# Splitting k and v at position 256, moving normalised x by 36 floats, and reordering work around it, in a stick-breaking decoder layer

## The chip, the cores and the metric

The kernel runs on one core of one Trainium2 chip. The metric is the device time of one execution in microseconds; the median of several runs counts.

## The reference

One decoder layer on 512 positions of 2048 channels, with 16 learned meta positions ahead of them, all in float32. `L` is 528.

```python
n = rmsnorm(h, g_mix)                       # (528, 2048)
q, k, v, gb, gc, u = split(n @ w_in)        # 1024 columns each
q, k = rmsnorm(q per head), rmsnorm(k per head)      # 8 heads x 128
z = q @ k.T / sqrt(128)                     # per head, strictly causal
log_pass = reverse_cumsum(log_sigmoid(-z)) - log_sigmoid(-z)
o_attn = exp(log_sigmoid(z) + log_pass) @ v
o_conv = gb * causal_dwconv(gc * u, 3 taps)
h = h + concat(rmsnorm(o_attn), rmsnorm(o_conv)) @ w_out
n2 = rmsnorm(h, g_ffn)
h = h + (silu(n2 @ w_gate) * (n2 @ w_up)) @ w_down   # 5632 wide
return h[16:]
```

## The kernel before

**Arithmetic.** Channels lie on the 128 partitions, positions on the free axis. Each float32 operand of a large product is split into a high part (`fp32r`, by ScalarE: a copy or `L201`, `L314`, `L372`) and the rest (by VectorE: `L202`, `L315`, `L373`). Each 128 x 128 block of a product takes three matmuls: high by high, high by rest, rest by high (`L301` to `L303`, `L778` to `L780`). The conv, gate/up and down products also save one multiplication in eight by a block scheme (seven block products in place of eight), which needs sums and differences of activations and of weights (`add_quads`, `L208`).

**Stages.** First q of head 0 and k of head 0 run side by side while x arrives and is split (`steps`), then v of head 0, then for heads 1 to 7: k, q, v. Attention of head h (`attend`) is spread between the k tiles of the next head's products by `after(n, work)`: work is called after n ticks, and a product gives a tick per k tile. Then channel group products of the conv stage, the output projection, the FFN's gate and up products, and the down products in four chunks.

**Weights.** `next_w` gives a product its next split weight piece and prepares pieces ahead (`prepare`: cast on ScalarE, subtract on VectorE, then the DMA issue on SyncE for the piece that will use the freed place). The first ten pieces are small ("first"), the following ones hold 8 k tiles ("wide"). `n_first` is 10; `S_AHEAD` is 2.

**Normalised x.** `n_parts` holds 32 tiles (high and rest of 16 k tiles), each of 576 floats; the position axis starts 4 floats into the tile. q reads positions 16 to 528, k and v read 0 to 264 and 264 to 528, each into a half of a two-bank PSUM tile. `halves` and `two` give the reads of both halves as one instruction. The PSUM pool `pp` has two such tiles, taken in turn.

**Mix steps.** The conv stage needs mixed blocks of x: `load_mix(k)` loads four blocks of 258 positions of the k tiles k and k + 8 into the tile `x_mix` (one buffer) by four DMAs on GpSimd's queue; `mix_x` scales them on ScalarE (`L460`), forms four differences on VectorE (`L462` to `L465`), splits them into two staging tiles and stores these to `mix_dram` by GpSimd's queue (`L470`). Staging tiles have two buffers, shared with the attention output of the heads (`st_o`). Before the conv stage `mix_dram` is loaded back (`L717`, `L750`).

**Order.** A planner takes the program with its own costs of each instruction and fills each engine's queue, by program order as priority; it can put an instruction far ahead of its place. `tc.high_priority()` raises a block; `tc.keep_in_program_order(i)` pins an instruction behind everything written before it for the same engine; `tc.issue_after(i)` puts what the block writes for i's engine behind i. Engines run their queues in order.

**End of the output projection.** For each output tile `residual`, `mixed_blocks` and `split_f` make the FFN's operands `acts`; the last tile (`i == KT - 1`) is on the way to the first FFN product. `h_scale` computes the FFN's norm within the first pair, its sum over channels on TensorE at `L661`.

## Time and profile before

| | |
|---|---|
| median of 3 runs | 2051.3 us (2051.23 to 2053.13) |
| profiled execution | 2049.99 us, its span 2048.3 us |
| granted TensorE clock over the span | 0.998 |
| busy: TensorE, VectorE, ScalarE, GpSimd | 99%, 85%, 52%, 19% |
| DMA traffic | 356.29 MB, mean 174 GB/s |

Rows of the timeline are: start in us from the span's start, duration, engine, line, operation, tile written and tiles read, shapes, count, and in brackets the idle time of the engine before it with what ended it. The views by line give busy us, mean ns of one, and idle time before. Stretches give, after the bounds, the length and then busy us and instruction count of PE, PEld, DVE, ACT and POOL, the granted clock, the DMA share and GB/s. PE is TensorE's matmul, PEld its weight load, DVE VectorE, ACT ScalarE, POOL GpSimd, SP SyncE.

### The profile page before, as it was taken

The page shows a single profiled execution, that of the slowest core. Times are in us where ns is not written, and L with a number is a line of the kernel's source. Part 1 is how long each engine was busy: PE and PEld are TensorE (multiplying, and loading weights), DVE is VectorE, ACT ScalarE, POOL GpSimd, SP SyncE. Part 2 cuts the span into 40 slices and gives each one's busy share as a digit, 9 for nine tenths or more (in the row PEclk, how much of TensorE's full clock was granted, in tenths as well). Part 3 has the DMA queues.
Part 4 walks back from the last instruction along what each step waited for, and adds up shares of the span by engine and source line. Part 5 has one row for each costly group of instructions (what it writes and reads, how often), then busy time and mean ns, then how long its engine had stood idle before and what let it go on. Part 6 is the DMA issues. An engine that isn't in the chain of part 4 may idle for free.

```text
span 2048.3 us, 39668 instructions
## 1 busy us (share of the span) xinstructions
PE 2031.4 (99%) x16134; PEld 1966.7 (96%) x16134; DVE 1743.4 (85%) x2227; ACT 1066.5 (52%) x1535; POOL 382.8 (19%) x571
## 2 busy tenths in 40 slices
PE   9999999999999999999999999999999999999999
PEld 8989999999998888999999999999999999999999
DVE  8878887688887778999888888988988978888888
ACT  7666666444454435555555555555555544444443
POOL 1122222200004441111011011111111242131211
PEclk9999999999999999999999999999999999999999
DMA  7243343643355555556465465465455899798864
GB/s 261 83 134 120 118 134 125 222 139 103 114 187 171 168 167 181 156 174 176 149 175 159 141 176 163 136 176 170 135 173 167 264 343 347 177 305 206 215 149 93
DMA packets 153287, 356.29 MB, mean 174 GB/s; under 512 B 13888, under 2 KB 63808, under 8 KB 152336
## 3 DMA queue, kind: packets, MB, share of 16 engines
q1 hardware_dynamic: 67456, 212.50, 32.1%
q0 software_dynamic: 85648, 141.26, 25.7%
q8 instruction: 126, 2.06, 0.4%
q14 instruction: 57, 0.47, 0.1%
HBM read 275.78 MB, written 77.92 MB: 173 GB/s over the span
## 4 chain that ended last, share of the span: by engine, by line
PE 89%; DMA 4%; DVE 3%; issue 1%; ACT 1%; POOL 1%; SPq 0%; DVEq 0%; ACTq 0%; POOLq 0%
PE x L778 13%; PE x L779 13%; PE x L780 13%; PE z L778 6%; PE z L779 6%; PE z L780 6%; PE y L778 3%; PE y L780 3%; PE y L779 3%; PE pv L301 1%; PE pv L302 1%; PE pv L303 1%; DMA sw_in<-w_down 1%; PE pq L303 1%; PE pq L301 1%
## 5 line engine op out<-in xcount | busy, mean ns | idle before, releaser
L201 ACT CAST sw_split<-sw_in 128x1024 fp32r<-128x1024 f32 (+2 forms) x668 | 662.1, 992 | 715.9 <-PE z L779 188.6
L202 DVE TENSOR_TENSOR sw_split<-sw_in,sw_split 128x1024 fp32r<-128x1024 f32 (+2 forms) x668 | 770.0, 1153 | 153.1 <-ACT sw_split L201 145.7
L778 PE MATMUL x<-f,sw_split 128*128 128x256 f32 x1408 | 388.3, 276 | 0.2 <-ACT sides L802 0.2
L780 PE MATMUL x<-f,sw_split 128*128 128x256 f32 x1408 | 387.9, 276 | 0.1
L779 PE MATMUL x<-f,sw_split 128*128 128x256 f32 x1408 | 387.9, 275 | 0.0
L778 PEld LDWEIGHTS x<-f,sw_split 128*128 128x128 f32 x1408 | 265.0, 188 | 0.6 <-ACT sides L802 0.4
L780 PEld LDWEIGHTS x<-f,sw_split 128*128 128x128 f32 x1408 | 264.9, 188 | 0.4 <-DVE sw_split L202 0.4
L779 PEld LDWEIGHTS x<-f,sw_split 128*128 128x128 f32 x1408 | 265.0, 188 | 0.1
L1032 POOL DMA_DIRECT2D fd<-s x147 | 103.7, 918 | 713.6 <-DVE s L315 691.6
L208 DVE TENSOR_TENSOR sw_in<-sw_in 128x1024 f32<-128x1024 f32 (+1 forms) x164 | 187.9, 1146 | 12.0 <-DMA sw_in<-w_gu 3.2
L779 PE MATMUL z<-f,sw_split 128*128 128x256 f32 x704 | 193.7, 275 | 1.9 <-DVE f L315 1.9
L778 PE MATMUL z<-f,sw_split 128*128 128x256 f32 x704 | 193.7, 275 | 1.0 <-ACT sides L800 1.0
L780 PE MATMUL z<-f,sw_split 128*128 128x256 f32 x704 | 193.6, 275 | 0.0
L780 PE MATMUL x<-ring,sw_split 128*128 128x256 f32 x608 | 167.3, 275 | 0.5 <-DVE sw_split L202 0.5
L778 PE MATMUL x<-ring,sw_split 128*128 128x256 f32 x608 | 167.2, 275 | 0.0
L779 PE MATMUL x<-ring,sw_split 128*128 128x256 f32 x608 | 167.2, 275 | 0.0
L779 PEld LDWEIGHTS z<-f,sw_split 128*128 128x128 f32 x704 | 132.2, 188 | 2.0 <-DVE f L315 2.0
L778 PEld LDWEIGHTS z<-f,sw_split 128*128 128x128 f32 x704 | 132.1, 188 | 1.2 <-ACT sides L800 1.2
L780 PEld LDWEIGHTS z<-f,sw_split 128*128 128x128 f32 x704 | 132.2, 188 | 0.0
L780 PEld LDWEIGHTS x<-ring,sw_split 128*128 128x128 f32 x608 | 114.1, 188 | 0.7 <-DVE sw_split L202 0.7
L778 PEld LDWEIGHTS x<-ring,sw_split 128*128 128x128 f32 x608 | 114.1, 188 | 0.0
L779 PEld LDWEIGHTS x<-ring,sw_split 128*128 128x128 f32 x608 | 114.1, 188 | 0.0
(611 smaller groups left out, 5511.9 us busy)
## 6 DMA issues: line engine op xcount, KB each, us to landing
sw_in<-w_gu SPq DMA_DIRECT2D x176, 512.0 KB, 3.9
sw_in<-w_in SPq DMA_DIRECT2D x92, 512.0 KB, 3.3
fd<-s POOLq DMA_DIRECT2D x147, 256.0 KB, 5.2
sw_in<-w_down SPq DMA_DIRECT2D x96, 384.0 KB, 4.4
ring<-fd POOLq DMA_DIRECT2D x42, 768.0 KB, 16.6
sw_in<-w_out SPq DMA_DIRECT2D x32, 512.0 KB, 3.5
out_T<-d POOLq DMA_DIRECT2D x54, 256.0 KB, 5.6
mix_dram<-st_x POOLq DMA_DIRECT2D x32, 258.0 KB, 2.9
```

The costliest lines, as they stand in the source:

```text
L201: sc.copy(hi, src)
L202: ve.tensor_tensor(lo, src, hi.bitcast(F32), ALU.subtract)
L208: return ve.tensor_tensor(sums[name], a, b, ALU.add)
L301: pe.matmul(ps, wh, ah[:, a:b], start=k + i == 0, stop=False)
L302: pe.matmul(ps, wh, al[:, a:b], start=False, stop=False)
L303: pe.matmul(ps, wl, ah[:, a:b], start=False, stop=k + i == last)
L778: pe.matmul(p, hi[:, kk], ah, start=start and j == k == 0, stop=False, skip_group_check=skip)
L779: pe.matmul(p, hi[:, kk], al, start=False, stop=False, skip_group_check=skip)
L780: pe.matmul(p, lo[:, kk], ah, start=False, stop=k == n - 1, skip_group_check=skip)
L1032: gp.dma_start(fd[c][s][:, :, k], t[:, :, i])
```

## The change

Normalised x starts 40 floats into its tiles in place of 4. k and v (and k's sum of squares) are cut into positions 0 to 256 and 256 to 528; the first part goes to the second half of the first PSUM bank, the second part to the start of the next bank, so that both lie side by side and are read as one run of 528. Weight pieces 11 and 12 (from 0) are prepared after the reads of q of head 0 have been put into ScalarE's queue. The load of the first mix step is written after head 1's product and pinned there, each following load at the end of the mix step before it; mix step k is written in head k + 2 in place of k + 1, and steps 6 and 7 in the first two conv products. The last two splits of the last output tile are raised like the rest of that tile's work.

```diff
@@ -269,9 +269,15 @@
                     load_quad(SIX + 1, QUADS[1])
 
     def next_w():
-        ahead = max(min(n_first, used[0] + 6), used[0] + 1 + S_AHEAD - (used[0] == n_first))
+        ahead = max(min(n_first, used[0] + 6), used[0] + 1 + S_AHEAD)
+        if used[0] < n_first:
+            ahead = min(ahead, n_first + 1)
         while len(split_w) < min(len(pieces), ahead):
-            prepare()
+            if n_first < len(split_w) <= n_first + S_AHEAD:
+                with tc.issue_after(read_q0[3].ins):
+                    prepare()
+            else:
+                prepare()
         used[0] += 1
         return split_w[used[0] - 1]
 
@@ -340,7 +346,7 @@
 
 
     H = L // 2
-    n_parts = [[npool.tile([P, L + 48], F32R, name=f"{t}{k}")[:, 4:] for t in ("nh", "nl")] for k in range(KT)]
+    n_parts = [[npool.tile([P, L + 48], F32R, name=f"{t}{k}")[:, 40:] for t in ("nh", "nl")] for k in range(KT)]
     npool.tile([P, 52], F32, name="pad_n")
     n_hl = []
     accs = [rpool.tile([P, L], F32, name=f"acc_x{i}") for i in range(2)]
@@ -381,8 +387,11 @@
             sc.activation(s, xts[k], AF.Square)
             ve.tensor_tensor(accs[k % 2], accs[k % 2], s, ALU.add)
 
-    def halves(ps, n):
-        return ps[:, :, :n]
+    def flat(ps):
+        return ps.rearrange("p a b -> p (a b)")[:, T2 : T2 + L]
+
+    def parts_of_all(ps):
+        return [(ps[:, 0, T2:], 0, T2), (ps[:, 1, : L - T2], T2, L)]
 
     def two(t):
         return t.rearrange("p (a b) -> p a b", a=2)
@@ -391,15 +400,14 @@
 
         raw = t512(L, "e", 2)[:, :cols]
         s = t512(L, "e2", 2)[:, :cols]
-        raw_v, s_v = (raw, s) if cols == SEQ else (two(raw), two(s))
-        sc.activation(s_v, ps, AF.Square)
-        last = sc.activation(raw_v, ps, AF.Copy, scale=g)
+        sc.activation(s, ps, AF.Square)
+        last = sc.activation(raw, ps, AF.Copy, scale=g)
         return raw, s, cols, last
 
     pk0 = pp.tile([P, 2, 512], F32, tag="pp", name="pk0")
     pq0 = pp.tile([P, 2, 512], F32, tag="pp", name="pq0")
     steps = [
-        product_steps([(pk0[:, 0, :H], 0, H), (pk0[:, 1, :H], H, L)], n_hl, KT),
+        product_steps(parts_of_all(pk0), n_hl, KT),
         product_steps([(pq0[:, 0, :], META, L)], n_hl, KT),
     ]
 
@@ -417,7 +425,7 @@
             split_x(k)
         for step in steps:
             next(step)
-    read_k0, read_q0 = read_qk(halves(pk0, H), g_k, L), read_qk(pq0[:, 0, :], gq_s, SEQ)
+    read_k0, read_q0 = read_qk(flat(pk0), g_k, L), read_qk(pq0[:, 0, :], gq_s, SEQ)
     for k in range(6):
         square_x(k)
     with tc.issue_after(read_k0[3].ins):
@@ -447,15 +455,19 @@
     def stage(name):
         return stpool.tile([P, 4 * N], F32R, tag="st_o", bufs=2, name=name)
 
+    xs = {}
+
     def load_mix(k):
-        x = xpool2.tile([P, 4, N], F32, tag="x", name=f"x_mix{k}")
+        xs[k] = xpool2.tile([P, 4, N], F32, tag="x", name=f"x_mix{k}")
         for m in range(4):
             at = C0 + m % 2 * T2
-            gp.dma_start(x[:, m], xT[k + m // 2 * 8][:, at : at + N])
-        return x
-
-    def mix_x(k, x):
-
+            load = gp.dma_start(xs[k][:, m], xT[k + m // 2 * 8][:, at : at + N])
+            if not k:
+                tc.keep_in_program_order(load)
+
+    def mix_x(k):
+
+        x = xs[k]
         for i in range(2):
             sc.activation(x[:, 2 * i : 2 * i + 2], x[:, 2 * i : 2 * i + 2], AF.Copy, scale=g_mix[:, k + 8 * i : k + 8 * i + 1])
         a0, a1, b0, b1 = (x[:, m] for m in range(4))
@@ -468,13 +480,15 @@
             split(st[:, :, 0], st[:, :, 1], x[:, m : m + 2])
             for i, block in enumerate(blocks):
                 gp.dma_start(mix_dram[block][:, k], st[:, i])
+        if k < 7:
+            load_mix(k + 1)
 
     def qk_norm(read, dst, parts_of, name):
 
         raw, s, cols = read[:3]
         sh = apool.tile([P, L], F32R, tag="sh", name=f"sh_{name}")[:, :cols]
         sl = apool.tile([P, L], F32R, tag="sl", name=f"sl_{name}")[:, :cols]
-        cuts = [(0, cols)] if cols == SEQ else [(0, H), (H, L)]
+        cuts = [(0, cols)] if cols == SEQ else [(0, T2), (T2, L)]
         split(sh, sl, s)
 
         def finish():
@@ -500,30 +514,31 @@
 
         if h:
             pk = pp.tile([P, 2, 512], F32, tag="pp", name=f"pk{h}")
-            product([(pk[:, 0, :H], 0, H), (pk[:, 1, :H], H, L)], n_hl)
-        read = read_qk(halves(pk, H), g_k, L) if h else read_k0
+            product(parts_of_all(pk), n_hl)
+        read = read_qk(flat(pk), g_k, L) if h else read_k0
         kn = kns[0]
         kh = apool.tile([P, 384], F32R, tag="kh", name=f"kh{h}")
         kl = apool.tile([P, 384], F32R, tag="kl", name=f"kl{h}")
         after(8 if h else 19, qk_norm(read, kn[:, :L], (kh, kl, 384), f"k{h}"))
 
         if h:
-            x = load_mix(h - 1)
             pq = pp.tile([P, 2, 512], F32, tag="pp", name=f"pq{h}")
             product([(pq[:, 0, :], META, L)], n_hl)
         read = read_qk(pq[:, 0, :], gq_s, SEQ) if h else read_q0
         qn = apool.tile([P, SEQ], F32, tag="qn", name=f"qn{h}")
         qh = apool.tile([P, SEQ], F32R, tag="qh", name=f"qh{h}")
         ql = apool.tile([P, SEQ], F32R, tag="ql", name=f"ql{h}")
-        if h:
-            after(5, lambda: mix_x(h - 1, x))
+        if h > 1:
+            after(5, lambda: mix_x(h - 2))
         after(9 if h else 22, qk_norm(read, qn, (qh, ql, SEQ), f"q{h}"))
 
         pv = pp.tile([P, 2, 512], F32, tag="pp", name=f"pv{h}")
-        product([(pv[:, 0, :H], 0, H), (pv[:, 1, :H], H, L)], n_hl)
+        product(parts_of_all(pv), n_hl)
         vt = t512(L, "e", 2)
         with tc.high_priority(0 if h else 1 << 20):
-            ve.tensor_tensor(two(vt[:, :L]), halves(pv, H), two(r), ALU.mult)
+            ve.tensor_tensor(vt[:, :L], flat(pv), r, ALU.mult)
+        if h == 1:
+            load_mix(0)
         after(6 if h else 15, lambda: attend(h, kn, kh, kl, qn, qh, ql, vt))
 
     def attend(h, kn, kh, kl, qn, qh, ql, vt):
@@ -680,8 +695,8 @@
         square_sum(acc_c, p, j == 0, s, ve)
         sc.activation(p, p, AF.Copy, scale=g_cnv[:, j : j + 1])
 
-    x = load_mix(7)
-    after(3, lambda: mix_x(7, x))
+    after(3, lambda: mix_x(6))
+    after(19, lambda: mix_x(7))
     pc = cu_product("pc0")
     cu0 = t512(L, "e", 2)[:, : SEQ + 2]
     ve.tensor_tensor(cu0[:, :T2], pc[:, 0, :T2], r2[:, C0 : C0 + T2], ALU.mult)
@@ -976,8 +991,8 @@
                 residual(ve)
                 mixed_blocks()
                 square_sum(acc_h, hj, False, wide_tmp("h", bufs=2), ve)
-            split_f(3, 5)
-            split_f(4, 6)
+                split_f(3, 5)
+                split_f(4, 6)
         else:
             residual(gp if half else ve)
             if half:
```

## The prediction

> **What bounds the kernel now.** First the page: the span, the busy shares, the chain that ended last.
>
> ```profile
> span 2048.3 us, 39668 instructions
> PE 2031.4 (99%) x16134; PEld 1966.7 (96%) x16134; DVE 1743.4 (85%) x2227; ACT 1066.5 (52%) x1535; POOL 382.8 (19%) x571
> PE 89%; DMA 4%; DVE 3%; issue 1%; ACT 1%; POOL 1%; SPq 0%; DVEq 0%; ACTq 0%; POOLq 0%
> ```
>
> TensorE sets the time: 99% busy and 89% of the chain. So an edit pays in two ways only: matmuls follow each other more closely, or a gap of TensorE (and the slow clock behind it) goes. Matmul ends are modelled, so I read pace from start to start in the timeline of PE, between two rows of a stretch without gaps.
>
> ```profile
> 35.07 0.28 PE L301 MATMUL pv<-nh,sw_split 128*128 128x264 f32 x1
> ...
> 43.81 0.28 PE L301 MATMUL pv<-nh,sw_split 128*128 128x264 f32 x1
> ...
> 387.18 0.39 PE L301 MATMUL pb<-nh,sw_split 128*128 128x512 f32 x1
> ...
> 397.58 0.39 PE L301 MATMUL pb<-nh,sw_split 128*128 128x512 f32 x1
> ...
> 614.54 0.39 PE L757 MATMUL po0z<-oc_hi,sw_split 128*128 128x512 f32 x1
> ...
> 617.26 0.39 PE L757 MATMUL po0z<-oc_hi,sw_split 128*128 128x512 f32 x1
> ...
> 902.78 0.28 PE L778 MATMUL z<-f,sw_split 128*128 128x256 f32 x1
> ...
> 905.50 0.28 PE L778 MATMUL x<-f,sw_split 128*128 128x256 f32 x1
> ```
>
> Steps between them: 72, 45, 12 and 24. So k and v's 264 columns take 8.74/72 = 121.4 ns, normalised x's 512 columns 10.40/45 = 231.1 ns, the output projection's 512 columns 2.72/12 = 226.7 ns, the FFN's 256 columns 2.72/24 = 113.3 ns. Per column: 0.460, 0.451, 0.443, 0.443. The first two read normalised x; the others do not. In the program of before, weights start at byte 128 modulo 256, the output projection's operands at 128, the FFN's at 240; k and v's two parts start at 176 and 208, q at 240. The change adds 36 floats: q comes to 128, equal to its weights, and both new parts of k and v to 64.
>
> **The change part by part.** Counts first, from the groups by line and the rows of the tile pb; then one row of the conv stage.
>
> ```profile
> L301 PE MATMUL pk<-nh,sw_split 128*128 128x264 f32 x256 | 73.9, 289 | 0.2 <-ACT nh L372 0.2
> L301 PE MATMUL pv<-nh,sw_split 128*128 128x264 f32 x256 | 73.8, 288 | 1.6 <-ACT tmp L396 1.6
> L301 PE MATMUL pq<-nh,sw_split 128*128 128x512 f32 x128 | 50.6, 395 | 0.0
> ...
> L301 PE MATMUL pb<-nh,sw_split x32: 392/392/501, 373.7 to 397.6; 128*128 128x512 f32 x32
> ...
> L779 PE MATMUL x<-nl,sw_split 128*128 128x258 f32 x168 | 47.9, 286 | 1.1 <-DMA nl<-mix_dram 1.1
> ```
>
> *q's start.* Three lines: 3 x 128 for q and 3 x 32 for pb (same start), 480 matmuls. Pace of the equal-start row instead of now: 4.4 ns each, **-2.1 us**. Bounds: 0 (start doesn't matter) and 2.1.
>
> *k and v in 256 + 272.* 3 x 512 matmuls are 768 pairs of 242.8 ns, 528 columns. Ends: FFN's pace, 233.7 ns, saves 9.1 ns or 7.0 us; today's pace saves nothing. I take the pace of the same tiles at 512 columns, 0.451, as the nearest row: 238.3 ns, **-3.5 us**. A loss is not excluded: 264 columns are 4.5 ns off the FFN's pace (264 x 0.443 = 116.9), and if start 64 costs as much again, it is +6.9. No row has this start.
>
> [...] The two rows of 512 columns disagree: 231.1 against 226.7. [...]
>
> *Conv operands* of normalised x move with it (unmixed 258-column blocks). Their mean duration of 286 sits in the same band as 264's 288 and they hold their lengths; I cost them at nothing, and +-1 us in the range.
>
> *Reads of k and v as one flat run* keep their element counts: nothing.
>
> *First projections to v (about 32 us).* ACT and PE timelines, then the start.
>
> ```profile
> 29.75 2.97 ACT L201 CAST sw_split<-sw_in 128x1024 fp32r<-128x1024 f32 x3 [1.77 <-DMA sw_in<-w_in]
> ...
> 33.13 0.69 ACT L396 ACTIVATE tmp<-pk,vec 128x528 f32<-128x528 f32 x1
> ...
> 33.88 0.39 PE L301 MATMUL pv<-nh,sw_split 128*128 128x264 f32 x1 [1.62 <-ACT tmp L396]
> 59.91 0.63 PE L533 MATMUL va<-ident,tmp 128*128 128x128 f32 x4 [0.64 <-DVE tmp L526]
> ...
> 2.81 2.19 POOL L454 DMA_DIRECT2D x_mix<-xT  x4
> ...
> 16.96 1.33 ACT L460 ACTIVATE x_mix<-x_mix,vec 128x516 f32<-128x516 f32 x2
> ...
> PEld pk L302 <- DVE nl L373: 3.3, 8, 0.7
> ...
> 4.00:8.00 4.00, 3.77 (x17) 2.56 (x15) 2.28 (x5) 3.01 (x7) 1.00 (x2) 1.00 0.95 271
> ```
>
> pv0 takes pk0's PSUM buffer, so it waits for L396's read of it, and that stands behind three weight casts of 0.99 us. The change leaves one cast ahead and puts the next two behind q0's read. The read comes 1.98 us earlier, more than the 1.62 us of waiting: **-1.6 us** (bounds 0.5 and 1.8). The moved casts feed weights needed after the first piece of pv0, 48 matmuls x 121.4 = 5.8 us later; at two casts plus VectorE's part (about 3.5 us after the reads) that covers them. What is queued behind them is the squares, with x_scale due a whole product later.
>
> The first mix load and step ran in the start: four DMAs at 2.81, scaling at 16.96, although written for head 1. Now they come after head 1's product. The DMA queues were 0.95 busy at 271 GB/s in the 4:8 row and TensorE waited for nl; four blocks of 128 x 258 floats are 0.53 MB, 1.9 us of transfer at that rate. Bounds 0 and 1.9, I take **-1.0**, the middle, since part of the waits for nl come from ACT's and VectorE's own work. The second step's VectorE part leaves 44 to 46 us too, ahead of the read that va waits for at 59.91: **-0.6** (0 to 0.6).
>
> *Mix steps of the heads.* Tile x_mix, POOL and ACT timelines, busy time by stretch around the gap:
>
> ```profile
> 114.46 2.17 POOL L454 DMA_DIRECT2D x_mix<-xT  x4
> ...
> 121.55 0.73 ACT L460 ACTIVATE x_mix<-x_mix,vec 128x516 f32<-128x516 f32 x1 [4.73 <-DMA x_mix<-xT]
> ...
>   DMA x_mix<-xT: 4.7, 1
> ...
> DMA to landing us min/median/max: 3.2/3.8/6.5
> ...
> 124.62:128.03 3.41, 1.47 (x8) 0.95 (x7) 3.41 (x6) 2.68 (x6) 0.15 (x1) 1.00 0.43 136
> 128.03:131.45 3.42, 3.42 (x15) 3.25 (x15) 3.11 (x5) 1.57 (x2) 0.14 (x1) 0.50 0.06 20
> ```
>
> One load of eight made ACT, which runs in order, stand 4.73 us; TensorE then idled 3.41 - 1.47 = 1.94 us, and ran the next 3.42 us at clock 0.50, 1.71 us more: 3.65 us in one place. The change issues each load at the end of the mix step before and uses it a head later, so the load is old when ACT comes to it: **-3.65** (bounds 0 and 3.65). [...] POOL's queue gets the same loads and stores in another order: the load waits for the buffer that its store has just read, and masks of the next softmax stand behind it as they do now.
>
> *Tail.* Two mix steps instead of one lie beside the last products.
>
> ```profile
> 350.77 1.06 POOL L470 DMA_DIRECT2D mix_dram<-st_x  x2 [3.53 <-DVE st_x L315]
> ...
> 388.11 0.57 POOL L750 DMA_DIRECT2D nl<-mix_dram  x1 [0.75 <-PE pb L303]
> ```
>
> The last store is out at 350.77, its readers start at 388.11: 37 us of cover. One more step of 16 k-tiles (96 x 121.4 = 11.7 us) and a load (6.5 at most) use 18 of it: nothing. With the cover gone each us late is a us, since TensorE's next wait there is for these loads.
>
> *FFN start.*
>
> ```profile
> 793.34 1.23 DVE L208 TENSOR_TENSOR sw_in<-sw_in 128x1024 f32<-128x1024 f32 x1 [3.08 <-DMA sw_in<-w_gu]
> 794.48 0.75 DVE L315 TENSOR_TENSOR f<-src,f 128x256 fp32r<-128x256 f32 x2
> ...
> 794.96 0.39 PE L779 MATMUL z<-f,sw_split 128*128 128x256 f32 x1 [1.85 <-DVE f L315]
> 797.03 0.79 PE L661 MATMUL ss_h<-work_r,ones_r 128*128 128x512 f32 x1 [1.00 <-DVE work_r L315]
> ...
> 793.62:797.03 3.41, 1.08 (x7) 0.84 (x7) 3.41 (x6) 1.05 (x1) 0.00 (x0) 1.00 0.22 89
> 797.03:800.46 3.43, 3.43 (x15) 3.34 (x16) 2.98 (x5) 1.26 (x2) 0.00 (x0) 0.50 0.02 5
> ```
>
> The last two splits stand on VectorE behind an add that waits 3.08 us for weights. Moved ahead, the 1.85 us wait goes. But work_r is late next: it stays behind the same add and gains only the 0.75 us of the two splits, so TensorE waits there about 2.1 us instead of 1.00: **-0.7 us**. Idle stays over the 1.94 us that halved the clock at 128 us, so I keep the slow stretch; if it goes, 1.7 more.
>
> Sum: 2.1 + 3.5 + 1.6 + 1.0 + 0.6 + 3.65 + 0.7 = 13.2 us. The profiled execution took 2049.99 us (1.7 beside its span), so 2036.8; the median of the runs is 1.3 above it: **2038**.
>
> **Rivals.**
> 1. *The stall in head 2 comes again, in another place.* For: what pins ACT's scaling is the planner's guess of the landing, and loads landed up to 6.5 us late; it hoisted steps by almost a head before. Against: seven of eight didn't wait. 13.2 - 3.65 = 9.5: 2041.8.
> [...]
> 3. *Slower: ACT stands before every mix step.* Only the first load is pinned to its place; loads issued earlier let the planner hoist the scaling of the following step into stretches where the load has not landed. A block costs 3.65; without that term the change gains 9.5, so it decides from the third block on (11.0), and at five of the heads 2 to 7 it is 18.3 - 9.5 = 8.8 above: 2060. Against: one wait in sixteen scalings now.
> 4. *The planner puts the moved work back*, starts lose at k and v what q gains: within 4 us of 2051.
>
> **How the numbers follow.** Forecast 0.53, rival 1 0.16, rival 2 0.13, rival 3 0.11, rival 4 0.07. A difference under 0.2% (4.1 us) can't be told from none here. Faster 0.53 + 0.16 + 0.13 = 0.82, same 0.07, slower 0.11. Low end: k and v at the FFN's pace (3.5 more), clock kept at 797 us (1.7), start 0.9 and 2 for what else gets earlier: 2030. High end: rivals 1 and 2 together leave 3.9 us, 2047.4, and a us of conv: 2048.5.
>
> **What would show it.** Right: PE starts of a pair of pk about 238 ns apart, q's 227; pv L301 without its wait on ACT; no L460 wait on x_mix; clock 1.00 over 117 to 159 us; z L779 without a wait on f but ss_h with a longer one. Wrong: pairs at 243 or above; L460 waiting several times; POOL's n-part loads starting later than 388; x_mix loads still in the first 10 us.

## The result: 2048.5 us, and the profile after

The changed kernel takes 2048.54 us (median of 20 runs, 2045.14 to 2053.02), the kernel before 2050.81 in the runs beside it: ratio 0.9987, 95% interval 0.9981 to 0.9993. That is 2.3 us less, where 13.2 were forecast, and 0.04 us above the range's upper end. The profiled execution took 2045.49 us, near the fastest of its runs, while that of before lay near its median; so the two traces differ by 4.5 us and not by 2.3. Runs that were granted a lower clock took longer: those of after whose granted clock rounds to 1.000 took 2045.3 us on average (2 runs), those at 0.997 took 2051.6 (2 runs).

The page of after: the span, the busy shares, the chain.

```profile
span 2043.8 us, 39672 instructions
...
PE 2025.8 (99%) x16134; PEld 1963.5 (96%) x16134; DVE 1742.3 (85%) x2227; ACT 1065.3 (52%) x1535; POOL 385.5 (19%) x571
...
PE 92%; DMA 3%; DVE 2%; ACT 1%; issue 1%; POOL 1%; SPq 0%; DVEq 0%; ACTq 0%; POOLq 0%
```

TensorE bounds the kernel as before. PE's timeline of after gives the pace, from start to start:

```profile
31.83 0.28 PE L307 MATMUL pv<-nh,sw_split 128*128 128x256 f32 x1
...
34.66 0.29 PE L307 MATMUL pv<-nh,sw_split 128*128 128x272 f32 x1
...
37.62 0.28 PE L307 MATMUL pv<-nh,sw_split 128*128 128x256 f32 x1
...
80.06 0.28 PE L308 MATMUL pv<-nl,sw_split 128*128 128x256 f32 x1
...
82.67 0.28 PE L307 MATMUL pv<-nh,sw_split 128*128 128x272 f32 x1
...
384.26 0.39 PE L307 MATMUL pb<-nh,sw_split 128*128 128x512 f32 x1
...
394.92 0.39 PE L309 MATMUL pb<-nh,sw_split 128*128 128x512 f32 x1
```

24 matmuls lie between the first two rows and 24 between the next two: 256 columns take 2.83/24 = 117.9 ns, 272 columns 2.96/24 = 123.3. A pair is 241.2 ns: 242.8 before, 238.3 forecast. The fourth and fifth rows are the same tile and shape in head 1, 23 steps: 113.5 ns. The last two rows, 47 steps: 226.8 ns, as forecast (226.7); but q itself, between the attention's matmuls, averages 228.6 over all its steps without a wait (230.6 before).

What TensorE waited for in after (total us, times, longest):

```profile
PE x L795 <- DVE sw_split L202: 2.5, 2, 2.0
PE ss_q L498 <- ACT sh_q L320: 2.1, 1, 2.1
PE x L793 <- ACT sides L813: 1.5, 1, 1.5
PE va L548 <- DVE tmp L539: 1.4, 1, 1.4
PE z L793 <- ACT sides L815: 1.3, 1, 1.3
...
PE pk L307 <- ACT nh L378: 1.0, 1, 1.0
...
PE z L563 <- ACT qh L320: 0.4, 1, 0.4
```

The wait of pv for ACT is gone, that of va has grown from 0.64 to 1.4, and head 2 still has one on q's sum of squares. The timelines of POOL, ACT and PE show how that one comes about, then the stretches (last columns: granted clock, DMA share, GB/s):

```profile
89.54 2.41 POOL L464 DMA_DIRECT2D x_mix<-xT  x4
...
93.44 0.73 ACT L472 ACTIVATE x_mix<-x_mix,vec 128x516 f32<-128x516 f32 x1 [3.40 <-DMA x_mix<-xT]
...
114.22 2.14 POOL L482 DMA_DIRECT2D mix_dram<-st_x  x4
116.35 2.16 POOL L464 DMA_DIRECT2D x_mix<-xT  x4
118.50 0.33 POOL L581 TENSOR_SCALAR_AFFINE_SELECT lw<-lw 128x128 f32<-128x128 f32 x1
...
118.86 0.53 ACT L320 CAST wh<-lw 128x400 fp32r<-128x400 f32 x1 [2.38 <-POOL lw L581]
...
121.79 1.44 ACT L472 ACTIVATE x_mix<-x_mix,vec 128x516 f32<-128x516 f32 x2 [1.45 <-DMA x_mix<-xT]
...
123.66 0.58 ACT L403 ACTIVATE tmp<-pq 128x512 f32<-128x512 f32 x1
...
126.24 0.80 PE L498 MATMUL ss_q<-sh_q,ones_r 128*128 128x512 f32 x1 [2.08 <-ACT sh_q L320]
```

```profile
122.70:126.10 3.40, 1.46 (x13) 1.26 (x11) 2.02 (x4) 3.15 (x7) 0.57 (x1) 1.00 0.48 154
126.10:129.50 3.40, 3.26 (x12) 2.73 (x13) 3.30 (x7) 1.45 (x3) 0.00 (x0) 0.50 0.00 0
```

The planner took the first mix step, that of head 2, up while k's product of that head ran (86.7 to 104.6 us); its place in the program is in v's product, which begins at 117.5. Its scaling at 93.44 waits 3.40 us for the load issued at 89.54. TensorE loses little by it, 0.39 us where z waits for q's cast (`qh`): without the early step ACT stands 3.02 us there anyway, for TensorE (e11). The step's four stores and the next step's four loads then hold POOL's queue for 4.3 us ahead of a mask, and ACT waits 2.38 us for that mask. Then ACT scales the next step's blocks, also early, and waits 1.45 us for the load issued at 116.35. q's read stands behind both. TensorE idles 1.94 us of the first stretch, and the next runs at clock 0.50: the picture of before, from another releaser. In before the mask stood behind stores and loads as well, but it was not held up by them:

```profile
122.84 0.29 POOL L566 TENSOR_SCALAR_AFFINE_SELECT lw<-lw 128x128 f32<-128x128 f32 x1 [6.21 <-ACT lw L618]
```

POOL had been idle for 6.21 us when it came, since ACT, which makes the mask's input, itself stood in its wait for the load up to 121.55.

The later steps don't wait, but their loads are not old either. The fourth step's load and scaling in after:

```profile
183.05 2.16 POOL L464 DMA_DIRECT2D x_mix<-xT  x4
...
188.60 0.71 ACT L472 ACTIVATE x_mix<-x_mix,vec 128x516 f32<-128x516 f32 x1
```

The load comes 5.55 us before its scaling; in before it came 5.57 us before (184.53 and 190.10). `x_mix` has one buffer, and the step before reads it up to its last split on VectorE (181.02 to 181.7 us here); only then, behind the step's last two stores (182.00), is the next load issued. From the third step on the planner puts the scaling some 5.5 us behind the load.

The traces compared by stretches, from the first matmul into one PSUM tile to the first into another, worked out from PE's timelines. e1, e2, e13 and e18 are runs of the next section.

| us | before | after | e1 parts | e2 order | e13 | e18 |
|---|---|---|---|---|---|---|
| pk0 to pk1 (start) | 40.61 | 37.76 | 41.07 | 37.44 | 37.83 | 37.55 |
| pk1 to va0 | 13.58 | 15.11 | 13.59 | 15.17 | 15.27 | 12.99 |
| va0 to pq2 | 45.63 | 46.05 | 45.76 | 46.99 | 46.29 | 46.36 |
| pq2 to pk3 (head 2) | 31.55 | 31.33 | 31.11 | 31.72 | 28.46 | 28.00 |
| pk3 to pc0 (5 heads) | 209.12 | 207.82 | 207.81 | 209.12 | 208.36 | 207.81 |
| pc0 to y10 | 431.53 | 430.73 | 430.90 | 431.90 | 432.63 | 431.40 |
| y10 to y12 (FFN start) | 59.76 | 58.60 | 61.09 | 60.14 | 58.66 | 58.83 |
| y12 to the last matmul | 1206.63 | 1206.60 | 1206.75 | 1206.68 | 1206.86 | 1206.68 |

The row pc0 to y10 holds a wait for the loads of the mixed blocks that differs between profiles with the same order of work (0.15 us in after at 408.6, 2.10 in e8 at 411.4), so differences of 2 us in it say nothing of an edit.

### The profile page after: what moved, and what is told of

It is laid out like the page before. It is cut to its first block, busy times and chain, and to the rows that moved or that the text cites. A ratio compares the mean times of both kernels' runs of the same rounds, so it can differ in the third digit from the quotient of the medians.

```text
span 2043.8 us, 39672 instructions
## 1 busy us (share of the span) xinstructions
PE 2025.8 (99%) x16134; PEld 1963.5 (96%) x16134; DVE 1742.3 (85%) x2227; ACT 1065.3 (52%) x1535; POOL 385.5 (19%) x571
## 4 chain that ended last, share of the span: by engine, by line
PE 92%; DMA 3%; DVE 2%; ACT 1%; issue 1%; POOL 1%; SPq 0%; DVEq 0%; ACTq 0%; POOLq 0%
PE x L795 13%; PE x L793 13%; PE x L794 13%; PE z L794 6%; PE z L793 6%; PE z L795 6%; PE y L795 3%; PE y L793 3%; PE y L794 3%; PE pv L307 1%; PE pv L308 1%; PE pv L309 1%; PE pq L309 1%; PE pq L308 1%; PE pq L307 1%; PE pk L307 1%
```

## The experiments

Runs of one kernel spread over up to 8 us, more than any single term; so a term is read from its stretch, and the medians say whether the sum holds.

### The two halves of the change: e1_parts and e2_order

Layout alone, in the kernel before:

```diff
-[:, 4:] for t in ("nh", "nl")]
+[:, 40:] for t in ("nh", "nl")]
-product_steps([(pk0[:, 0, :H], 0, H), (pk0[:, 1, :H], H, L)], n_hl, KT),
+product_steps(parts_of_all(pk0), n_hl, KT),     # and so for k, v, their reads and k's sum of squares
```

> The kernel before with only the layout of the change: normalised x 36 floats further on (q's operands start at 128 modulo 256, as their weights do), k and v in parts of 256 and 272 positions, read as one run. No order of work is changed. Theory (starts matter, but less than forecast): the traces of before and after give 241.1 against 243.0 ns for a pair of k's matmuls, and a mean of about 228.6 against 231.1 ns for q's 512 columns; 768 pairs x 1.9 = 1.5 us and 480 x 2.5 = 1.2 us, so 2.7 us less than before (ratio 0.9987), and the stretch at clock 0.50 near 128 us stays as in before. As forecast (4.4 ns and 4.5 ns): 5.6 us less (0.9973). Rival (starts do not matter, what the two traces differ by is disturbance): no change.

Reorderings alone, in the changed kernel:

```diff
-[:, 40:] for t in ("nh", "nl")]
+[:, 4:] for t in ("nh", "nl")]
-product(parts_of_all(pk), n_hl)
+product([(pk[:, 0, :H], 0, H), (pk[:, 1, :H], H, L)], n_hl)
```

> The changed kernel with the old layout (offset of 4 floats, k and v in two halves of 264 positions read as two blocks): the reorderings alone. As forecast: 1.6 + 1.0 + 0.6 + 3.65 + 0.7 = 7.5 us less than before. Theory from the two traces: the start gains about 2.9 us, of which 1.5 goes back where the transposes of head 0's v wait for VectorE and 0.6 where z waits; the stall of head 2 stays with another releaser (about 2 us of idle TensorE and 3.4 us at clock 0.50): 1 to 2 us less than before (0.999). Rival (the layout and the order work against each other, so that the order alone brings its full sum): 0.9963.

Measured: e1 2047.08 us, ratio 0.9991 (0.9981 to 1.0); e2 2050.09, 0.9998 (0.9989 to 1.0007). The intervals of e1 and e2 overlap; by the stretches, all that the change is worth is the layout. The table says where the order's part went: e2's start is 3.17 us shorter than before's (2.6 were forecast for the first projections and the moved mix step), pk1 to va0 is 1.59 longer, va0 to pq2 1.36 longer, head 2 0.17 longer. The sum is 0.05 us less than before. The layout shows in every steady head: 41.56 us instead of 41.82, in e1 as in after.

### What sets the pace: e9_pace, e10_entry, e6_start240, e3_start128, e15_turns

Streams of matmuls alone; in `e9_pace` 48 of each width at each start, the other engines idle (starts are the program's addresses modulo 256, the weights' is 128; the profile shows no addresses). The code is shortened:

```diff
+for cols, c in ((512, "a"), (256, "b"), (264, "c"), (272, "d"), (258, "e")):
+    for o in range(0, 64, 4):              # 16 bytes apart; the second letter of the tile: a is 0, e 64, i 128, p 240
+        run(f"{c}_at_{chr(97 + o // 4)}", cols, o, 48)
```

> Only streams of matmuls, nothing of the layer is computed: weights start at 128 modulo 256; 48 matmuls each of 512, 256, 264, 272 and 258 columns with operands at 0, 16, 32 ... 240 modulo 256, other engines idle; then 512 columns with other matmuls in between; then 96 matmuls of 512 columns at 128 and at 0 with VectorE, ACT or POOL working beside them. Theory (the start against the weights sets the pace): 226.7 ns for 512 columns at 128 and about 231 at 240; 256 columns 113.3 at 240 and 117.6 at 64; 272 columns about 123.5 at 64; 264 columns about 121.5 at 176 and 208. Rival (disturbance by matmuls in between sets it): the same pace at all starts, and 230 or more in the stretches with other matmuls in between. Rival (other engines reading SBUF): the same pace at all starts, slower only beside VectorE or ACT.

First rows of six streams in PE's timeline; each next stream begins 48 matmuls later.

```profile
121.26 0.40 PE L65 MATMUL a_at_i<-xh,whi 128*128 128x512 f32 x1
...
132.18 0.39 PE L65 MATMUL a_at_j<-xh,whi 128*128 128x512 f32 x1
...
198.99 0.39 PE L65 MATMUL a_at_p<-xh,whi 128*128 128x512 f32 x1
...
210.08 0.28 PE L65 MATMUL b_at_a<-xh,whi 128*128 128x256 f32 x1
...
232.82 0.28 PE L65 MATMUL b_at_e<-xh,whi 128*128 128x256 f32 x1
...
238.28 0.28 PE L65 MATMUL b_at_f<-xh,whi 128*128 128x256 f32 x1
```

512 columns at 128: 10.92/48 = 227.5 ns (226.8 over the last 40); at 240: 11.09/48 = 231.0. 256 columns at 64: 5.46/48 = 113.8, and 113.3 once settled. So the start does matter, with nothing else running. But nearness to the weights' start is not the rule: 512 columns reach 226.7 at 112 and 128 only (229.1 to 234.5 at the other 14 starts), 256 columns 113.3 at 64 and 240 only (116.7 to 120.0 elsewhere, 120.0 at 128, the weights' own), 264 columns never less than 120.0, 272 never less than 123.3 (at 48, 64 and 240, at 32 once settled). Beside VectorE or ACT, 512 columns at 128 settle at 226.7 too: the rival on other engines is out. With a 272-column matmul after every third, the three between step by 230.0 ns (0.69 us for three, eleven times from 631.80 us), and by 226.7 again behind the last.

256 columns at 64 at 113.3: the kernel has that start and runs at 117.9. `e10_entry` repeats the kernel's sequence, 24 of one part and 24 of the other, with the kernel's places in PSUM (loops written out):

```diff
+pieces("new_e", new, 16)                                             # 256 and 272 at 64, as after
+pieces("low_e", [(0, 0, 0, 256), (1, 0, 256, 528)], 16)              # 256 at the start of a bank
+pieces("old_l", old, 44)                                             # 264 and 264 at 176 and 208, as before
+pieces("new_p", new, 60)                                             # 256 and 272 at 240
+pieces("one_e", new, 16, 1)                                          # the parts in turn, one matmul each
+pieces("daj_e", new, 16, before=(0, 192, 16))                        # a 192-column matmul ahead of each 256 part
+pieces("quarters_e", [(0, 0, 0, 256), (1, 0, 256, 512)], 16)         # 256 and 256 at 64
```

> Only streams of matmuls again, nothing of the layer is computed: 24 matmuls of one part, 24 of the other, in turn, as k and v run them (weights at 128 modulo 256, PSUM as in the kernel). In the last streams 256 columns at 64 ran at 113.3 ns, in the changed kernel's k at 117.7, and in its pv of head 1 at 113.3, where another matmul came in between. Theory (one start has several steady paces, and what came before decides which one a stretch falls into): 256 at 64 runs at 117.7 behind 272 at 64 here too, and at 113.3 behind a short other matmul of some width; parts taken turn about every 3 or every matmul give yet another pace. Rival (the place in PSUM decides: second half of a bank in the kernel, start of a bank in the last streams): 117.7 with the kernel's place, 113.3 with the 256 part at a bank's start, whatever comes before. Rival (the other engines' work in the kernel): 113.3 in all of these. For the two halves of 264 at their old starts (176 and 208, letter l): 121.7 and 121.2.

```profile
66.62 0.29 PE L65 MATMUL new_e<-xh,whi 128*128 128x272 f32 x1
...
69.58 0.28 PE L65 MATMUL new_e<-xh,whi 128*128 128x256 f32 x1
...
72.41 0.29 PE L65 MATMUL new_e<-xh,whi 128*128 128x272 f32 x1
...
990.36 0.28 PE L65 MATMUL quarters_e<-xh,whi 128*128 128x256 f32 x1
...
1012.14 0.28 PE L65 MATMUL quarters_g<-xh,whi 128*128 128x256 f32 x1
```

Steps of 24, 24 and 192: 123.3 ns, 117.9 ns (2.83/24), and 113.4 for 256 behind 256. The kernel's pair, 241.2 above, comes out as 241.1 here; old_l gives 242.7, the pair of before (242.8). The place in PSUM made no difference (low_e: 241.1). A 192-column matmul ahead of each 256 part lets it settle at 113.3 (pair 238.5), which costs 89 ns for 24 matmuls that gain 2.6 each: a loss. So 256 columns at 64 ran at more than one steady pace, 117.9 over all 24 behind 272 columns and 113.4 over 192 behind 256, with nothing changed but what ran before; in pv of head 1 a matmul of the attention stood just ahead of the stretch (at 79.87 us), by chance, and it ran at 113.5. Shown is this behaviour; what in the engine makes it is not. The cut at 256 is not the only way to this pace: halves of 264 columns at other starts, 16 and 48 (old_b) or 48 and 80 (old_d), take 240.6 and 240.5 a pair in the streams. No kernel was run with them.

Three kernels with other layouts test the streams as a table. `e6_start240` and `e3_start128` move normalised x:

```diff
-[:, 40:] for t in ("nh", "nl")]
+[:, 20:] for t in ("nh", "nl")]      # e6: k and v at 240, q at 48; e3: 8 and 48 floats of padding ahead, k and v at 128, q at 192
```

> The changed kernel with normalised x 20 floats lower: both parts of k and v start at 240 modulo 256 and q at 48, so that no start equals the weights' 128. By the streams (512 columns: 226.7 ns at 128, 233.3 at 48; 256 columns: 113.3 at 64 and 240; 272 columns: 123.3 at 64 and 240): q loses 233.3 - 228.6 = 4.7 ns x 480 = 2.3 us against the changed kernel; k and v gain (117.7 + 123.4) - (113.3 + 123.3) = 4.5 ns x 768 = 3.5 us if 256 columns fall into their fast pace there, as the FFN's do at 240: together 1.2 us less than the changed kernel. Rival (the slow pace of 256 columns comes behind 272 at 240 too): 2.3 us more than the changed kernel, about the time of before. As forecast (distance from the weights' start sets the pace): q at 231 or more, k and v no better than at 64: 1 to 5 us more than the changed kernel.

> The changed kernel with normalised x moved so that both parts of k and v start at 128 modulo 256, equal to their weights, and q at 192. By the forecast's rule (equal start is the good one): k and v at 238 ns a pair or less, 2 us less than the changed kernel there, q at 229 to 231: about 1 to 2 us less in all (0.998). By the streams (256 and 272 in turn at 128: 244.7 a pair; 512 columns at 192: 229.1): (244.7 - 241.1) x 768 = 2.8 us more for k and v, 0.2 more for q: about 3 us more than the changed kernel, 1.0002 of before.

`e15_turns` takes the parts in turn:

```diff
-for n_part, (ps, a, b) in enumerate(parts):
-    for i, (wh, wl) in enumerate(ws):
+for i, (wh, wl) in enumerate(ws):
+    for ps, a, b in parts:
+        pe.matmul(ps, wh, ah[:, a:b], start=k + i == 0, stop=False)
...                                     # the same for wh with al, and for wl with ah
```

> The changed kernel with the two parts of k and v taken turn about, one matmul of 256 columns and one of 272 with the same weights, instead of 24 and 24. By the streams (one_e against new_e): a pair 240.0 ns instead of 241.1, 0.8 us less in 768 pairs. Rival (the attention's matmuls between them, and products whose parts now end together, cost more than that): the changed kernel's time or up to 2 us more.

| | pair of k and v, ns | streams | q, ns | a steady head, us | ratio |
|---|---|---|---|---|---|
| after | 241.0 | 241.1 | 228.6 | 41.56 | 0.9987 |
| e6 (240 and 48) | 240.3 | 239.7 | 232.9 | 41.69 | 0.9990 (0.9981 to 0.9998) |
| e3 (128 and 192) | 244.8 | 244.7 | 229.9 | 41.98 | 0.9994 (0.9985 to 1.0003) |
| e15 (in turn) | 240.3 | 240.0 | 228.7 | 41.60 | 0.9977 (0.9968 to 0.9986) |

Kernel and streams agree within 0.3 ns, in e6 within 0.6. e6's expectation was missed: 256 columns at 240 come down to 113.3 only within their 24 matmuls (e10's new_p: 115.4 on average, 113.3 over the last 12), so k and v gain 0.8 ns a pair and not 4.5, and q loses more than they gain: a steady head takes 0.13 us more. e3, equal starts for k and v, is the worst: the forecast's rule is refuted there. e15 gains in the pair what it loses elsewhere in the head, and no stretch explains its ratio; I read nothing from it.

### The stall of head 2: e5_pin, e11_pin0, e13_tie1, e17_tie_ln_vt

`e5_pin` ties every mix step behind its own head's read of q:

```diff
+with tc.issue_after(read[3].ins):      # read: this head's read_qk of q
     mix_x(h - 2)
```

> The changed kernel, but each mix step (scaling, mixing, stores, and the load of the next) is tied behind its own head's read of q from PSUM, so that it can't be taken up a head early. Theory (in head 2 four stores and four loads of a step taken up early stand on the POOL queue ahead of a mask, and the scaling of the next step, early too, waits for its load; both hold ACT, and TensorE waits for q's sum of squares): the wait of 2.1 us and the stretch at clock 0.50 near 126 us go, 3.5 to 4 us less than the changed kernel, about 6 less than before (0.997). Rival (the steps lie beside attention wherever they are put, and the wait only moves to a later head): time of the changed kernel, 2.3 less than before (0.9988), with a stretch at clock 0.50 in another head. Rival (ACT has no room there and every head loses a little): slower than the changed kernel.

e5's stretch of head 2, then what TensorE waits for in e5's tail, 335 to 375 us:

```profile
117.00:160.00 43.00, 43.00 (x298) 40.38 (x297) 34.68 (x60) 29.13 (x48) 10.08 (x23) 1.00 0.39 123
```

```profile
PE z L567 <- ACT qh L320: 1.1, 1, 1.1
PE z L567 <- DVE v L559: 0.6, 1, 0.6
```

43 us busy at clock 1.00: the stall is gone, 27.35 us from pq2 to pk3 instead of 31.33, 4.0 us. But the kernel takes 2051.67 us, 1.0005 (0.9996 to 1.0014): head 4 gives 1.9 back, 3.1 go in the tail, where the last steps, a head later than the planner had them, meet the last attention, and 1.5 at the start of the FFN, where this profile has a spell of slow clock (0.94 on average from 780 to 810 us). The theory on the place held, its sum didn't.

`e11_pin0` ties only the first step (`if h == 2`).

> The changed kernel with only the first mix step, that of head 2, tied behind its head's read of q; the later ones are left where they stood (from head 4 on the order on ACT is that of the changed kernel). Theory (tying all steps took 4.3 us out of head 2 and gave 1.9 back in head 4, 3.1 in the tail, where the last steps came too late): the 4.3 us of head 2 stay gone and nothing is given back, 4.3 less than the changed kernel, about 6.5 less than before (0.9968). Rival (the second step, with its load now issued behind the first, waits for that load in head 3 as it did in head 2): 0.9985 to 0.9988.

Measured 2046.01 us, 0.9974 (0.9963 to 0.9985). Head 2 keeps 27.35; the rival's price comes true in head 3, 43.86 us instead of 41.55, but not by its mechanism. The second step's scaling (133.65 us) waits for no load; its differences on VectorE stand ahead of the copy of v for which z waits 0.64 us (at 138.62). The third step's scaling, hoisted into the same head, is the one that meets its load (2.3 us of ACT's waiting, from 159.3 us). `e13_tie1` leaves the first step and POOL's order alone and ties only the second, behind head 2's read of q (`if h == 3`):

> The changed kernel with only the second mix step tied behind head 2's read of q; the first stays a head early, and POOL's queue keeps its order, four stores and four loads ahead of the mask. It tells apart the two waits that hold ACT in head 2 of the changed kernel. Theory (the scaling that waits for its load, 1.45 + 1.44 us ahead of q's read, is what makes TensorE late by 2.1 us): the wait for q's sum of squares and the slow clock go, pq2 to pk3 takes 27.4 us instead of 31.3, about 3.9 less than the changed kernel, less what a wait of the same scaling costs in head 3 (up to 2.3 by the run with the first step tied): 0.9970 to 0.9981 of before. Rival (POOL's stores and loads ahead of the mask, 2.38 us of ACT's waiting, are enough by themselves): pq2 to pk3 stays at 31.3, time of the changed kernel (0.9987).

ACT's timeline of e13, then its stretch of head 2:

```profile
119.48 0.53 ACT L320 CAST wh<-lw 128x400 fp32r<-128x400 f32 x1 [2.39 <-POOL lw L588]
...
123.39 0.59 ACT L403 ACTIVATE tmp<-pq 128x512 f32<-128x512 f32 x1
123.88 0.68 ACT L404 ACTIVATE tmp<-pq,gq_s 128x512 f32<-128x512 f32 x1
124.96 0.73 ACT L472 ACTIVATE x_mix<-x_mix,vec 128x516 f32<-128x516 f32 x1
```

```profile
117.00:160.00 43.00, 42.15 (x286) 38.85 (x285) 35.04 (x62) 28.44 (x49) 12.09 (x27) 1.00 0.50 157
```

The mask still makes ACT wait 2.39 us, yet the stall is down from 31.33 to 28.46 us and the clock stays at 1.00. So the scaling ahead of q's read carries 2.9 us. Of the 1.1 that are left above e5's 27.35, 0.58 are waits for the same sum of squares (0.35 and 0.23), which fits ACT's wait for the mask; no run takes POOL's queue out alone. Head 3 gives 0.55 back (42.10 us), 0.26 of it in a wait of z for `ql` at 139.16. The first step's scaling waits 3.58 us for its load here too (at 94.05), and z 0.57 behind it. In all 2044.87 us, 0.9969 (0.9958 to 0.9981).

`e17_tie_ln_vt` ties the first step behind head 2's read of q and each later one behind the logarithms of the attention before, and moves head 0's scaled v (below).

> The changed kernel with head 0's scaled v in the mix loads' buffer, the first mix step tied behind head 2's read of q, and each later one behind the logarithms of the attention of the head before its own, which is where the planner puts the steps from head 4 on, so that none is made up for in a hurry and each load has nearly a head to land. Theory (what costs time is a step taken up soon after its load was issued; where the steps are a head apart nothing waits): no wait of the scaling of x_mix in heads 2 to 7, heads at 41.56 us each from pk3 on, head 2 at 27.4 from pq2 to pk3, va without its wait: 4.0 + 1.4 = 5.4 less than the changed kernel, 0.9962 of before. Rival (the tied steps come too late for the tail, as with all steps tied behind q's read): pc0 to pu0 at 17.2 instead of 14.1, 2.3 less than the changed kernel, 0.9976.

Measured 2049.82 us, 0.9990 (0.9981 to 0.9999). Heads 4 to 7 run at 41.56 and head 2 at 27.5, but the rival decides, and at a higher price: pc0 to pu0 takes 20.60 us instead of 14.07. The seventh step's scaling waits 3.69 us for its load (at 339.88), va and z wait 3.0 us in all from 343 to 350, and 6.83 us run at half clock (0.71 and 0.61 on average over these stretches):

```profile
345.00:350.00 5.00, 3.42 (x12) 2.36 (x13) 4.27 (x9) 2.55 (x7) 0.75 (x2) 0.71 0.29 105
350.00:355.00 5.00, 5.00 (x28) 5.00 (x29) 0.41 (x2) 2.83 (x6) 3.56 (x7) 0.61 1.00 291
```

### Head 0's v: e12_pin0_vt

e11 with another buffer:

```diff
-vt = t512(L, "e", 2)
+vt = t512(L, "e", 2) if h else xpool2.tile([P, 4, N], F32, tag="x", name="vt0").rearrange("p a b -> p (a b)")
```

> The kernel with the first mix step tied, and head 0's scaled v put into the free buffer of the mix loads instead of one of the two that q's and k's reads use. Theory (the scaled v waits for a buffer that k's normalisation frees, so the transposes of v can't come earlier with v's product): the wait of va for VectorE, 1.41 us in the changed kernel, goes, and the start keeps it: about 1.4 less than with the tied step alone (0.9961 of before). Rival (the next wait of the start, z on the casts of q, takes it over): the same as with the tied step alone (0.9968), with z's waits longer by what va's are shorter.

The wait of va goes: pk1 to va0 is 12.98 us against 15.29 in e11. 0.9 of the 2.3 come back up to pq2, so 1.4 stay, as expected. The scaled v had waited for a buffer that k's normalisation frees. That the whole kernel is faster than e11 is not shown (2044.71, 0.9972, 0.9959 to 0.9984; the intervals overlap): its head 3 takes 45.35 us, with a wait of z for the copy of v (1.59 us) and a spell of slow clock (0.67 on average from 140 to 145 us).

### The start of the FFN: e8_f

```diff
                 square_sum(acc_h, hj, False, wide_tmp("h", bufs=2), ve)
-                split_f(3, 5)
-                split_f(4, 6)
+            split_f(3, 5)
+            split_f(4, 6)
```

> The changed kernel without its raise of the last two splits of f at the start of the FFN. From the profiles so far, the stretch from the last convolution pair's y10 to y12 took 59.8 and 61.1 us without the raise (two kernels), 58.4 to 60.8 with it (eight kernels). Forecast and theory: the raise is worth 0.7 us, so 0.7 us more than the changed kernel, z waits 1.9 for f and ss_h 1.0 again. Rival (the wait only changes its name: without the one for f, TensorE meets ACT's sides and VectorE's split of the weights at 793 to 803 us): the same time as the changed kernel within a us, whatever the waits are called.

Measured 2047.38 us, 0.9982 (0.9973 to 0.9991), not slower than the changed kernel. One stretch of after and one of e8:

```profile
794.00:801.00 7.00, 7.00 (x63) 7.00 (x62) 6.90 (x10) 1.84 (x3) 0.00 (x0) 1.00 0.36 114
```

```profile
794.00:801.00 7.00, 6.00 (x50) 5.75 (x49) 6.76 (x11) 3.23 (x4) 0.00 (x0) 1.00 0.27 94
```

e8 has the old waits back (z 1.6 for f, ss_h 1.0) and no slow clock: y10 to y12 takes 57.97 us, less than in any kernel with the raise (58.3 to 58.9 where the clock stays, up to 60.8 where it doesn't). Before's 59.76 less its 1.71 us of slow clock is 58.05, the same. So by these profiles the raise gains nothing, it costs 0.4 to 0.9 us. With it TensorE waits elsewhere: 1.99 us at 793.07 for VectorE's split of the weights and 1.55 at 805.69 for ACT (`sides`), two of the waits listed for after above. What moves this stretch more is whether the clock drops behind the idle time (0.50 from 797.03 to 800.46 us in before, 1.00 throughout in after), which is not settled by the edit: of the 11 profiles with the raise 6 had a slow spell here, of the 3 without it 2.

### Both losses taken out: e18_best

```diff
+with tc.high_priority(1 << 20):        # h == 2: the first step stays early
+    mix_x(0)
+with tc.issue_after(reads_q[2].ins):   # h == 3: the second behind head 2's read of q
+    mix_x(1)
...                                     # vt of head 0 in the buffer of the mix loads, as above
```

> The changed kernel with head 0's scaled v in the mix loads' buffer, the first mix step raised ahead of all other work of its time (it was a head early already; the new buffer had moved it), and the second tied behind head 2's read of q. Theory (the two losses of the changed kernel, the scaling that waits for a load just issued and the scaled v that waits for a buffer, are independent): from pk1 to pk3 about 2.9 + 1.2 less than the changed kernel, and the load of the second step, issued earlier now, lands before its scaling, 1.0 to 1.5 more: 4 to 5.5 less in all, 0.9960 to 0.9968 of before. Rival (raised work of the first step takes the attention's turn on VectorE and ACT in head 1): as much lost between pq1 and pk2 as is gained, time of the version with the second step tied alone (0.9969) or slower.

```profile
span 2039.5 us, 39671 instructions
...
PE 2024.0 (99%) x16134; PEld 1961.5 (96%) x16134; DVE 1743.0 (85%) x2227; ACT 1065.7 (52%) x1535; POOL 384.5 (19%) x571
```

```profile
112.00:172.00 60.00, 60.00 (x414) 56.03 (x413) 51.14 (x87) 39.96 (x67) 13.99 (x30) 1.00 0.38 119
```

Measured 2041.19 us (5 runs), 0.9957 (0.9944 to 0.9969): it beats both kernels. From 112 to 172 us (the end of head 2 and head 3) TensorE has no gap and no slow clock; pk1 to pk3 is 87.35 us against 92.49 in after, 5.1 less, where 5.1 to 5.6 were expected of the three pieces. The second step's load is issued at 107.30 and has landed at 113.23, well before its scaling at 120.79, as expected; the first step's scaling still waits 3.0 us for its load (at 93 to 95), which costs TensorE nothing here. pq2 to pk3 is 28.00 and not 27.35: q's product of head 2 takes 0.65 us longer, with the attention's matmuls spread in more places between its own.

## Why the prediction was wrong, step by step

Of the seven terms of the forecast's sum five were mis-sized or had the wrong sign.

- *Head 2, -3.65: the step that failed most.* Stretch pq2 to pk3: -0.22, of which the layout alone gives -0.44. The forecast said that each load is used a head after its issue and so is old when ACT comes to it. That held for no step: the loads come 3.9, 5.4 and then about 5.5 us before their scaling, since the one buffer is held by the step before and the planner puts the scaling close behind the load. The first scaling waited 3.40 us, the second 1.45, and the second one stood ahead of q's read. It is rival 1, which had 0.16; its time, 2041.8, missed through the other terms. The sentence that POOL's masks "stand behind it as they do now" was wrong too. In before two stores and four loads stood there as well, but the mask came 6 us later, behind ACT's own wait; in after ACT was in time, and four stores and four loads were in the mask's way. Rival 3's mechanism, steps hoisted into loads that have not landed, was there twice and cost TensorE a stall once, not five times. With the wait taken out (e5, e18) the stretch is 3.6 to 4.2 below before's, 3.1 to 3.8 without the layout's share, so the term's size was right.
- *k and v, -3.5:* 768 pairs x (242.8 - 241.0) = -1.4. The nearest row, 512 columns' pace per column, gave 238.3 ns for the pair and did not hold for this width. The FFN's 113.3, taken as the far end, is what 256 columns at this start can do (113.4 behind 256 in e10); behind 272 columns they ran at 117.9.
- *q's start, -2.1:* pb gains all of its 4.2 ns x 96 = 0.4; q gains 2.0 x 384 = 0.8, since the attention's matmuls between its own throw it off its pace, as the 272-column ones did in e9 (230.0 instead of 226.7). -1.2 in all. Direction right, and that starts don't matter to pace (rival 2, 0.13) is refuted: with nothing else running, e9's 512 columns take 226.7 ns at 128 and 231.0 at 240. That equal starts are the good ones is wrong: e3, with both parts of k and v at the weights' 128, takes 244.8 ns a pair. No start of e9 came below 226.7 for 512 columns.
- *First projections -1.6 and the mix step out of the start -1.0:* right in their sum; pv's wait for ACT is gone. pk0 to pk1: -2.85 in after, -3.17 in e2.
- *va, -0.6:* wrong sign, +1.5. The argument removed VectorE's mix step from ahead of it; the wait was for a buffer (e12), so TensorE, 2.9 us earlier, waits longer for a moment that came only 1.4 us earlier (va at 58.52 instead of 59.91). Another 0.4 goes where z waits for q's cast, behind the first step's scaling.
- *FFN, -0.7:* +0.4 to +0.9 (e8). The wait of z for f went, as forecast, but no longer wait of ss_h came in its place: TensorE meets the split of the weights and `sides` instead. In the one profile the gain of 1.2 is 1.7 of slow clock less about 0.6.
- *Conv, nothing:* about right; pc0 to pu0 is 0.2 shorter.
- *Tail, nothing:* right for this order; e5 and e17 show how close it lay: 3 to 6.5 us when the steps come a head later.

The terms as measured come to about what lies between the traces: -1.2 - 1.4 - 2.9 + 1.5 + 0.4 + 0.2 - 1.2 = -4.6, with +0.2 for head 2 without the layout's share (the start's -2.9 holds a little of the layout's) against -4.4. The range failed by a hair because its upper end allowed for two misses, head 2's 3.65 and the 5.6 of both layout terms, not for a start that gives its gain back.

That the medians differ by 2.3 us where the profiles differ by 4.5 fits the slow spells: the profile of before has two (from 128.0 and 797.0 us), that of after one (126.1), and a spell costs about 1.7 us (an estimate: 3.40 to 3.43 us at clock 0.50). What stays open: why the clock dropped behind idle time in some runs and not in others, and e15's ratio.

## What to carry to other kernels

A gain at a start is only kept if what is late next is also early: ask of the next wait whether it is for work that moves along or for a buffer, a load or another queue with a date of its own. Issuing a load earlier does not help if its consumer may be taken up earlier too (here the loads came 3.9 to 5.55 us before their scaling), and it can't be issued before its buffer is free (read up to 181.7 us, load issued at 183.05): look up when that is, tie the consumer and not only the load, and look at which instruction stands behind it in its engine's queue (here q's read at 123.66, behind a scaling that had waited 1.45 us). And a pace read from one width or in one sequence need not carry over to another (238.3 ns forecast for the pair, 241.2 measured): a short stream of the very sequence, 24 and 24 at the kernel's addresses, foretold the kernel's pace to 0.6 ns or better.

## What the runs showed of the hardware

- In e9 (fp32r matmuls with a weight load each, weights at 128, 16 starts from 0 to 240) the pace differed with the operand's start, and for each width in its own way: 512 columns took 226.7 ns at 112 and 128 and up to 234.5 elsewhere, 256 columns 113.3 at 64 and 240 and up to 120.0 elsewhere.
- In e10, 256 columns at 64 ran at 117.9 ns over all 24 matmuls of a stretch behind 272 columns, and at 113.4 over 192 behind 256 columns. At 240, behind 272 columns, they averaged 115.4 and were at 113.3 over the last 12 of their 24.
- After 3.40 us in which TensorE was idle for 1.94, the granted clock was 0.50 for the next 3.40 us (after, from 122.70); in before, after 3.41 us with 1.94 idle, it was 0.50 for 3.42 us (from 124.62). With 0.85 us idle over the 43 us of head 2 (e13) it was 1.00. The length of a gap alone did not decide: 1.66 us idle in head 2 of e1 went with a mean clock of 0.96 over 43 us, a wait of 1.99 us in after (793.07) and one of 2.24 in e18 (788.72) with 1.00.
- Eight DMA issues on POOL's queue took 4.30 us in after (from 114.22), and the mask behind them started at 118.50, when they were done; ACT waited 2.38 us for it.
- Behind ACT's waits q's read stood: in before ACT waited 4.73 us for a load, up to 121.55, and read q's product at 125.00, although the last of its matmuls had started at 117.87; in after it waited 1.45 us for a load, up to 121.79, and read q at 123.66.
